# First token pair's transposes inside the last token tile's post products, and held-back q halves ahead of the last score block

## The chip, the cores and the metric

The kernel runs on one core of one Trainium2 chip (trn2). The metric is device time in microseconds, the median of three runs; the profile is of one further execution.

## The reference

Two layers over 512 tokens of width 1024, all in float32. Each layer does three sub-blocks on a residual stream `h`, and each sub-block starts with an RMS norm (pre) and ends with an RMS norm and the residual add (post):

- `h += 0.5 * rms(swiglu(rms(h)))`, with an inner width of 2816;
- `h += rms(mixer(rms(h)))`. One input projection feeds a short gated convolution, a Conformer convolution, differential attention (4 heads, two softmax maps per head, one subtracted from the other with a learned weight) and forgetting attention (8 heads). Each branch is mapped to width 1024, the gated sum of the four goes through an output projection `w_o`;
- a second `h += 0.5 * rms(swiglu(rms(h)))`.

## The kernel before

**Numbers and products.** Every float32 operand is split into a high part (rounded, ACT) and a low part (the rest, DVE), and every product is three matmuls: high by high, low by high, high by low (`mm3`, L128; `by_tokens`, L216). Weights come as one stream of 512 KB chunks; each is loaded by SP into `raw` (3 buffers), split by ACT into `wh` (L100) and by DVE into `wl` (L101), 5 buffers each. A chunk is 8 blocks of 128x128.

**The boundary between two sub-blocks** (`boundary`, L235) ends one and starts the next. It is reached seven times; the first has no post part (`post is None`, the input is loaded instead) and the last no pre part. The five between have both and are what the change touches. In each:

1. The post products run by tokens: for the second half of the channels, the last `HOLD` = 8 steps of the contraction are done token tile by token tile (L325 to L333). A tile of 128 tokens takes 8 steps of three matmuls, 24 matmuls of 512 columns.
2. After a tile's products come `gained` (square sums on ACT, `yg` on DVE), `update` (a reciprocal root `nr` on POOL, then the new residual `h` on DVE) and `normed` (square sums of `h` on ACT, another `nr` on POOL, then the normed rows `u` on DVE, L250). This chain is run for the four tiles one after the other while PE works on the next tile.
3. `turned` (L253) transposes the rows `u` of a pair of token tiles to channels by tokens: 16 PE transposes of 128x128 into four PSUM banks `pt` (four transposes each), and from each bank two pairs of copies: high part `xh` (ACT, L153) and low part `xl` (DVE, L146), each 128x256. Eight pairs in all for a token pair.
4. `outer(k, c)` (L272) does the first products of the next sub-block: for channel block k and one half of the tokens, four weight blocks by three matmuls of 256 columns, 12 matmuls, accumulated in four PSUM banks `pf`.

The order in the program is: products and chain of the four token tiles; `turned` for tiles 0 and 1; `outer` k = 0 to 5 for the first half; `turned` for tiles 2 and 3; `outer` k = 6 and 7 for the first half; `outer` k = 0 to 7 for the second half.

**Differential attention** (L585 to L630) runs four heads. Per head, `weights_of(i)` for the query blocks i = 0 to 3 makes two score blocks, their row minima (DVE, L517) and exponentials (ACT), and combines the two maps of block i - 1 (`combine`, DVE, L593 to L598, which ends with `e` at L597). The next head's query projection `q_of` stands between blocks 1 and 2. It puts two DVE operations that make the low halves of q (`qlo`, 64x512 each, L482) on the list `late`; the list is emptied by `settle`, which the next call of `group` does when its products are issued (L138, L123). That is `k_of` after block 3, where `combine` of block 3 is on the list behind them. `transposed` (L521) then turns the weights `e` by PE.

**What sets the order.** The kernel is written in a framework that plans: instructions of one engine are issued in an order that its planner derives from program order, its own costs and the buffers that are free. Buffers of one name come from one pool (`s`: 59 slots of 128x512 in SBUF, from which `xh`, `xl`, `u`, `yg`, `sq` all come; `p`: the 8 PSUM banks). In the loop of the four heads DVE alone is held to program order (`manual_schedule`, L585). Each engine works through its queue in order.

Of the kernel before, what the change touches and what calls it, by code (L numbers as in the profile page):

```python
# [22 lines left out]
NQ = T // P  # L23
# [18 lines left out]
HOLD = 8  # L42
# [12 lines left out]
def build(tc, ws, x, vecs, gains, wdf, lamv, fb, consts, out):  # L55
# [3 lines left out]
    with ExitStack() as ctx:  # L59
# [13 lines left out]
        def nm(s):  # L73
            cnt[0] += 1
            return f"{s}{cnt[0]}"
# [28 lines left out]
        def block(desc):  # L104
            i = len(order)
            order.append(desc)
            if i % CB == 0:
                c = i // CB
                for n in range(c, min(c + AHEAD + 1, NBLK // CB) if len(order) > 4 * KD else 0):
                    if n not in ready:  # L110
                        load(n)
                cur[:] = ready[c]
            j = (i % CB) * P
            return cur[0][:, j:j + P], cur[1][:, j:j + P]
# [4 lines left out]
        def settle():  # L119
            while late:  # L120
                late.pop(0)()
# [87 lines left out]
        def tile4(name, l, k, c):  # L209

            for j in range(4):
                block((name, l, k, c + P * j))
            b0 = (len(order) - 4) % CB * P
            return cur[0][:, b0:b0 + T], cur[1][:, b0:b0 + T]

        def by_tokens(out, x, t, w, first, last):  # L216

            r = slice(t * P, (t + 1) * P)
            PE.matmul(out=out, lhsT=x[0][:, r], rhs=w[0], start=first, stop=False)  # L219
            PE.matmul(out=out, lhsT=x[0][:, r], rhs=w[1], start=False, stop=False)  # L220
            PE.matmul(out=out, lhsT=x[1][:, r], rhs=w[0], start=False, stop=last)  # L221
# [10 lines left out]
        def squares(src, col):  # L232
            S.activation(out=slot(F32, "sq"), in_=src, func=AF.Square, accum_out=col)

        def boundary(post, pre, first):  # L235

            xs, pf, blk = [], [], []  # L240
            stat = np_.tile([P, 16], F32, tag="stat", name=nm("stat"))

            def normed(t):

                for c in range(2):
                    squares(hs[t][c], stat[:, 8 + 2 * t + c:9 + 2 * t + c])
                r = rstd_of([stat[:, 8 + 2 * t + c:9 + 2 * t + c] for c in range(2)])
                us = [slot(F32, "u") for _ in range(2)]
                for c in range(2):
                    V.tensor_scalar(out=us[c], in0=hs[t][c], scalar1=r, scalar2=None, op0=ALU.mult)  # L250
                return us

            def turned(us, h):  # L253

                c = HALVES[h]
                for b in range(4):
                    p = ps("pt")
                    for i in range(2):
                        k = 2 * b + i
                        for t in range(2):  # L260
                            o = k % 4 * P
                            PE.transpose(out=p[:, i * H + t * P:i * H + (t + 1) * P],
                                         in_=us[t][k // 4][:, o:o + P], identity=ident)
                    for i in range(2):
                        k = 2 * b + i
                        if len(xs) <= k:
                            xs.append((slot(F32R, "xh"), slot(F32R, "xl")))
                        g = vcol(pre[0], pre[1], k)
                        hi_of(xs[k][0][:, c], p[:, i * H:(i + 1) * H], g)
                        lo_of(xs[k][1][:, c], p[:, i * H:(i + 1) * H], xs[k][0][:, c], g)  # L270

            def outer(k, c):  # L272

                if not pf:
                    pf.extend(ps("pf") for _ in range(4))
                if len(blk) <= k:
                    blk.append([block(first[f][k]) for f in range(4)])
                x = (xs[k][0][:, c], xs[k][1][:, c])
                for f in range(4):
                    mm3(pf[f][:, c], blk[k][f], x, k == 0, k == KD - 1)  # L280

            us = []
            if post is None:
                for t in range(4):
                    for c in range(2):
                        nc.sync.dma_start(out=hs[t][c], in_=x[t * P:(t + 1) * P, c * T:(c + 1) * T])
                    load(t, 2 if t == 0 else 1)
                us = [normed(t) for t in range(4)]
            else:
                row, factor, name, l, ys = post  # L290
                n = len(ys)
                gb = gp.tile([P, D], F32, tag="gb", name=nm("gb"))
                nc.scalar.dma_start(out=gb, in_=gains[row:row + 1, :].broadcast_to([P, D]))
                yg = [[None, None] for _ in range(4)]

                def gained(t, c, p):
                    squares(p, stat[:, 2 * t + c:2 * t + c + 1])
                    yg[t][c] = slot(F32, "yg")
                    V.tensor_mul(out=yg[t][c], in0=p, in1=gb[:, c * T:(c + 1) * T])

                def update(t):
                    r = rstd_of([stat[:, 2 * t + c:2 * t + c + 1] for c in range(2)], factor)
                    for c in range(2):
                        V.scalar_tensor_tensor(out=hs[t][c], in0=yg[t][c], scalar=r, in1=hs[t][c],
                                               op0=ALU.mult, op1=ALU.add)
                        if pre is None:
                            (nc.sync, nc.scalar)[c].dma_start(out=out[t * P:(t + 1) * P, c * T:(c + 1) * T],
                                                              in_=hs[t][c])

                settle()  # L310
                py = [ps("py") for _ in range(4)]
                for k in range(n):
                    w = tile4(name, l, k, 0)
                    for t in range(4):
                        by_tokens(py[t], ys[k], t, w, k == 0, k == n - 1)
                    cover()
                for t in range(4):
                    gained(t, 0, py[t])
                py = [ps("py") for _ in range(4)]
                for k in range(n - HOLD):  # L320
                    w = tile4(name, l, k, T)
                    for t in range(4):
                        by_tokens(py[t], ys[k], t, w, k == 0, False)
                held = []
                for t in range(4):  # L325
                    for k in range(n - HOLD, n):
                        if t == 0:
                            held.append(tile4(name, l, k, T))
                        by_tokens(py[t], ys[k], t, held[k - n + HOLD], k == 0, k == n - 1)
                    gained(t, 1, py[t])  # L330
                    update(t)
                    if pre is not None:
                        us.append(normed(t))  # L333
                if pre is None:
                    return None
            turned(us[0:2], 0)
            for k in range(KD - 2):
                outer(k, HALVES[0])
            turned(us[2:4], 1)
            for k in range(KD - 2, KD):  # L340
                outer(k, HALVES[0])
            for k in range(KD):
                outer(k, HALVES[1])
            pf.append(group(first[4], xs))
            pf.append(group(first[5], xs))
            return xs, pf
# [35 lines left out]
        def mixer(l, entry):  # L382
# [198 lines left out]
            q, k = q_of(OFF_CQ), k_of(OFF_CK)  # L581
# [3 lines left out]
            with tc.manual_schedule(engines={mybir.EngineType.DVE}):  # L585
                for hd in range(4):
# [13 lines left out]
                    def weights_of(i):  # L600
                        for m in range(2):
                            exponentials(scores(q, k, m, i, False), es[m][i], bias[:, (NQ - 1 - i) * P:],
                                         sums[i][:, m:m + 1])
                        if i:
                            combine(i - 1)
# [3 lines left out]
                    weights_of(1)  # L609
                    q_next = q_of(cq)  # L610
                    weights_of(2)
                    weights_of(3)
                    late.append(lambda: combine(NQ - 1))
                    k_next = k_of(ck)
                    q, k = q_next, k_next
# [73 lines left out]
            for pr in range(4):  # L689
# [35 lines left out]
                if pr < 3:  # L725
                    q, k = nxt
# [54 lines left out]
        post = None  # L781
        for l in range(DEPTH):
            post = ffn(l, 1, boundary(post, ("ffn1_pre_g", l), ffn_first(l, 1)))
            post = mixer(l, boundary(post, ("mix_pre_g", l), mix_first(l)))
            post = ffn(l, 2, boundary(post, ("ffn2_pre_g", l), ffn_first(l, 2)))
# [51 lines left out]
```

## Time and profile before

| | before |
|---|---|
| median of 3 runs | 2795.95 us (2794.83 to 2796.22) |
| profiled execution, its own time | 2795.68 us |
| its span in the trace | 2793.9 us |
| PE (matmul) busy | 2720.7 us, 97% |
| DVE busy | 1392.6 us, 50% |
| ACT busy | 980.0 us, 35% |
| POOL busy | 75.7 us, 3% |
| weights and other data moved | 257.82 MB, mean 92 GB/s |

The profiled execution lies 0.27 us below the median of the runs, and 1.78 us of its time lie outside the span. PE is busy for nearly the whole span, so what counts is the 73.2 us in which it isn't, and the stretches in which it is busy at a lower clock.

### The profile page before, as it was taken

The page shows a single profiled execution, that of the slowest core. Times are in us where ns is not written, and L with a number is a line of the kernel's source. Part 1 is how long each engine was busy: PE and PEld are TensorE (multiplying, and loading weights), DVE is VectorE, ACT ScalarE, POOL GpSimd, SP SyncE. Part 2 cuts the span into 40 slices and gives each one's busy share as a digit, 9 for nine tenths or more (in the row PEclk, how much of TensorE's full clock was granted, in tenths as well). Part 3 has the DMA queues.
Part 4 walks back from the last instruction along what each step waited for, and adds up shares of the span by engine and source line. Part 5 has one row for each costly group of instructions (what it writes and reads, how often), then busy time and mean ns, then how long its engine had stood idle before and what let it go on. Part 6 is the DMA issues. An engine that isn't in the chain of part 4 may idle for free.

```text
span 2793.9 us, 32240 instructions
## 1 busy us (share of the span) xinstructions
PE 2720.7 (97%) x12884; PEld 2280.1 (82%) x12884; DVE 1392.6 (50%) x2287; ACT 980.0 (35%) x1607; POOL 75.7 (3%) x114
## 2 busy tenths in 40 slices
PE   7999989999999989999989999899999999899999
PEld 6888878887888878888888888888878888788887
DVE  4333248776775443332343332496777854433322
ACT  4222232354453333222242222324545533332221
POOL 0000000000000000000000000000000000000000
PEclk9999999999999999999999999999999999999999
DMA  4222223222222222222222222222222222232221
GB/s 153 97 98 98 98 70 109 88 76 68 95 84 95 98 83 98 94 95 99 83 98 99 98 98 97 87 94 81 76 84 87 84 94 98 70 112 95 95 98 68
DMA packets 73494, 257.82 MB, mean 92 GB/s; under 512 B 8432, under 2 KB 8816, under 8 KB 73344
## 3 DMA queue, kind: packets, MB, share of 16 engines
q1 hardware_dynamic: 68688, 246.45, 26.5%
q10 hardware_dynamic: 4656, 9.32, 1.0%
q8 instruction: 101, 1.65, 0.2%
q14 instruction: 49, 0.40, 0.0%
HBM read 253.60 MB, written 2.13 MB: 92 GB/s over the span
## 4 chain that ended last, share of the span: by engine, by line
PE 95%; DVE 3%; POOL 1%; issue 1%; DMA 0%; ACT 0%; ACTq 0%; POOLq 0%; DVEq 0%; SPq 0%
PE p L130 21%; PE p L132 21%; PE p L131 21%; PE py L220 6%; PE py L221 6%; PE py L219 6%; PE pf L131 2%; PE pf L132 2%; PE pf L130 2%; PE o L545 1%; PE pv L219 1%; PE pv L221 1%; PE pv L220 1%; PE pt L529 1%; POOL nr L229 1%; PE sc L499 1%
## 5 line engine op out<-in xcount | busy, mean ns | idle before, releaser
L100 ACT CAST wh<-raw 128x1024 fp32r<-128x1024 f32 (+1 forms) x465 | 488.7, 1051 | 1417.4 <-PE p L131 664.9
L101 DVE TENSOR_TENSOR wl<-raw,wh 128x1024 fp32r<-128x1024 f32 (+1 forms) x465 | 567.8, 1222 | 765.3 <-ACT wh L100 752.9
L130 PE MATMUL p<-xh,wh 128*128 128x512 f32 x2304 | 903.1, 392 | 0.0
L132 PE MATMUL p<-xh,wl 128*128 128x512 f32 x2304 | 898.0, 390 | 0.0
L131 PE MATMUL p<-xl,wh 128*128 128x512 f32 x2304 | 897.7, 390 | 0.0
L132 PEld LDWEIGHTS p<-xh,wl 128*128 128x128 f32 x2304 | 433.0, 188 | 91.0
L131 PEld LDWEIGHTS p<-xl,wh 128*128 128x128 f32 x2304 | 433.4, 188 | 89.0 <-issue 0.5
L130 PEld LDWEIGHTS p<-xh,wh 128*128 128x128 f32 x2304 | 433.6, 188 | 88.5 <-PE pt L529 0.5
L221 PE MATMUL py<-wh,gl 128*128 128x512 f32 x704 | 273.9, 389 | 0.0
L219 PE MATMUL py<-wh,gh 128*128 128x512 f32 x704 | 273.9, 389 | 0.0
L220 PE MATMUL py<-wl,gh 128*128 128x512 f32 x704 | 273.9, 389 | 0.0
L363 DVE TENSOR_TENSOR s<-p,s 128x512 f32<-128x512 f32 x80 | 55.3, 692 | 270.6 <-PE p L132 270.6
L392 DVE SCALAR_TENSOR_TENSOR yc<-ba,vec,yc 128x501 f32<-128x501 f32 (+17 forms) x240 | 169.7, 729 | 2.4
L219 PEld LDWEIGHTS py<-wh,gh 128*128 128x128 f32 x704 | 132.1, 188 | 27.6
L220 PEld LDWEIGHTS py<-wl,gh 128*128 128x128 f32 x704 | 132.1, 188 | 27.4
L221 PEld LDWEIGHTS py<-wh,gl 128*128 128x128 f32 x704 | 132.1, 188 | 27.3
L130 PE MATMUL pf<-xh,wh 128*128 128x256 f32 x384 | 115.0, 304 | 30.3 <-ACT xh L153 30.3
L131 PE MATMUL pf<-xl,wh 128*128 128x256 f32 x384 | 115.9, 302 | 9.6 <-DVE xl L146 9.6
L132 PE MATMUL pf<-xh,wl 128*128 128x256 f32 x384 | 114.7, 299 | 0.0
L130 PEld LDWEIGHTS pf<-xh,wh 128*128 128x128 f32 x384 | 79.6, 210 | 31.9 <-ACT xh L153 31.9
L519 ACT ACTIVATE e<-e,mx 128x128 f32<-128x128 f32 (+3 forms) x128 | 71.2, 557 | 60.0 <-DVE mx L517 48.4
L131 PEld LDWEIGHTS pf<-xl,wh 128*128 128x128 f32 x384 | 80.2, 209 | 11.4 <-DVE xl L146 11.4
(185 smaller groups left out, 2623.1 us busy)
## 6 DMA issues: line engine op xcount, KB each, us to landing
raw<-ws SPq DMA_DIRECT2D x463, 512.0 KB, 3.3
cb<-cum ACTq DMA_DIRECT2D x16, 256.0 KB, 3.5
gb<-gains ACTq DMA_DIRECT2D x6, 512.0 KB, 4.7
h<-x SPq DMA_DIRECT2D x8, 256.0 KB, 5.6
out<-h SPq DMA_DIRECT2D x4, 256.0 KB, 2.0
out<-h ACTq DMA_DIRECT2D x4, 256.0 KB, 2.0
raw<-ws SPq DMA_DIRECT2D x2, 256.0 KB, 7.1
cst<-consts ACTq DMA_DIRECT2D x1, 384.0 KB, 4.8
```

The costliest lines, as they stand in the source:

```text
L100: S.copy(out=wh[:, j], in_=raw[:, j])
L101: V.tensor_sub(out=wl[:, j], in0=raw[:, j], in1=wh[:, j].bitcast(F32))
L130: PE.matmul(out=out, lhsT=w[0], rhs=x[0], start=first, stop=False)
L131: PE.matmul(out=out, lhsT=w[0], rhs=x[1], start=False, stop=False)
L132: PE.matmul(out=out, lhsT=w[1], rhs=x[0], start=False, stop=last)
L219: PE.matmul(out=out, lhsT=x[0][:, r], rhs=w[0], start=first, stop=False)
L220: PE.matmul(out=out, lhsT=x[0][:, r], rhs=w[1], start=False, stop=False)
L221: PE.matmul(out=out, lhsT=x[1][:, r], rhs=w[0], start=False, stop=last)
L229: G.tensor_tensor(out=r, in0=var, in1=mhalf[:, 0:1], op=ALU.pow)
L363: V.tensor_mul(out=u, in0=pu, in1=x)
L392: V.scalar_tensor_tensor(out=acc[:, s:], in0=y[:, :T - s], scalar=vcol(wname, l, i * 4 + j), in1=acc[:, s:], op0=ALU.mult, op1=ALU.add)
L519: S.activation(out=e, in_=e, func=AF.Exp, scale=-1.0, bias=mx, accum_out=sums)
```

## The change

In `boundary`, `turned` for token tiles 0 and 1 is called inside the products of token tile 3, after four of its eight steps, where there is a post and a pre part. Where there is no post part (the first boundary) it stays where it was. In the differential attention, `settle()` is called ahead of `weights_of(3)`, so that the two `qlo` operations on the list stand before block 3 on DVE.

```diff
                     for k in range(n - HOLD, n):
                         if t == 0:
                             held.append(tile4(name, l, k, T))
+                        if t == NQ - 1 and k == n - HOLD // 2 and pre is not None:
+                            turned(us[0:2], 0)
                         by_tokens(py[t], ys[k], t, held[k - n + HOLD], k == 0, k == n - 1)
                     gained(t, 1, py[t])
                     update(t)
@@
                 if pre is None:
                     return None
-            turned(us[0:2], 0)
+            if post is None:
+                turned(us[0:2], 0)
             for k in range(KD - 2):
                 outer(k, HALVES[0])
             turned(us[2:4], 1)
@@
                     weights_of(1)
                     q_next = q_of(cq)
                     weights_of(2)
+                    settle()
                     weights_of(3)
                     late.append(lambda: combine(NQ - 1))
                     k_next = k_of(ck)
```

## Rows read from the trace of the kernel before

**Rows 1.** The page: the chain of work that ended last, shares of the span by engine.

```profile
PE 95%; DVE 3%; POOL 1%; issue 1%; DMA 0%; ACT 0%; ACTq 0%; POOLq 0%; DVEq 0%; SPq 0%
```

**Rows 2.** Who waited for whom, PE's rows: engine, tile and line that waited, what for, us in total, times, longest.

```profile
PE pf L130 <- ACT xh L153: 30.3, 6, 5.6
PE pt L262 <- DVE u L250: 14.8, 2, 11.9
PE pt L529 <- DVE e L597: 11.5, 4, 3.6
PE pf L131 <- DVE xl L146: 9.6, 6, 1.7
```

**Rows 3.** The timeline of PE at the second boundary (first SwiGLU block to mixer, layer 0): start, duration, engine, line, instruction, count, and in brackets the idle time before it and what ended it.

```profile
381.78 0.39 PE L219 MATMUL py<-wh,gh 128*128 128x512 f32 x1
...
387.23 1.91 PE L262 MATMUL pt<-cst,u 128*128 128x128 f32 x16
394.77 0.79 PE L130 MATMUL pf<-xh,wh 128*128 128x256 f32 x2 [5.63 <-ACT xh L153]
397.26 0.58 PE L131 MATMUL pf<-xl,wh 128*128 128x256 f32 x1 [1.70 <-DVE xl L146]
...
403.56 0.28 PE L131 MATMUL pf<-xl,wh 128*128 128x256 f32 x1
...
408.47 1.91 PE L262 MATMUL pt<-cst,u 128*128 128x128 f32 x16
410.14 0.36 PE L130 MATMUL pf<-xh,wh 128*128 128x256 f32 x1
```

**Rows 4.** The same timeline at the four other boundaries that have a post and a pre part: the two sets of transposes of each.

```profile
1026.79 1.91 PE L262 MATMUL pt<-cst,u 128*128 128x128 f32 x16
...
1047.39 1.91 PE L262 MATMUL pt<-cst,u 128*128 128x128 f32 x16
...
1400.85 1.91 PE L262 MATMUL pt<-cst,u 128*128 128x128 f32 x16
...
1420.57 1.91 PE L262 MATMUL pt<-cst,u 128*128 128x128 f32 x16
...
1774.02 1.91 PE L262 MATMUL pt<-cst,u 128*128 128x128 f32 x16
...
1794.83 1.91 PE L262 MATMUL pt<-cst,u 128*128 128x128 f32 x16
...
2412.95 1.91 PE L262 MATMUL pt<-cst,u 128*128 128x128 f32 x16
...
2433.41 1.91 PE L262 MATMUL pt<-cst,u 128*128 128x128 f32 x16
```

**Rows 5.** Windows of the second boundary: from and to, length, then busy time and count of PE, PEld, DVE, ACT and POOL, the granted clock of TensorE (1.00 is 2.4 GHz, 0.50 is 1.2 GHz), share and rate of the DMA engines.

```profile
392.20:393.20 1.00, 0.00 (x0) 0.00 (x0) 1.00 (x2) 0.23 (x1) 0.00 (x0) 1.00 0.85 291
393.20:394.20 1.00, 0.00 (x0) 0.00 (x0) 1.00 (x2) 1.00 (x4) 0.00 (x0) 0.51 0.91 332
...
397.30:403.40 6.10, 6.10 (x28) 6.10 (x29) 3.11 (x7) 4.22 (x8) 0.00 (x0) 0.50 0.12 35
...
408.50:414.00 5.50, 5.50 (x50) 5.50 (x49) 3.41 (x8) 3.28 (x8) 0.00 (x0) 1.00 0.00 0
```

**Rows 6.** The timeline of DVE at the second boundary, in order of time.

```profile
381.85 0.88 DVE L250 TENSOR_SCALAR u<-h,nr 128x512 f32<-128x512 f32 x2 [0.73 <-POOL nr L229]
...
385.52 2.38 DVE L101 TENSOR_TENSOR wl<-raw,wh 128x1024 fp32r<-128x1024 f32 x2
...
388.24 1.22 DVE L101 TENSOR_TENSOR wl<-raw,wh 128x1024 fp32r<-128x1024 f32 x1
389.90 0.88 DVE L250 TENSOR_SCALAR u<-h,nr 128x512 f32<-128x512 f32 x2 [0.44 <-POOL nr L229]
390.70 0.68 DVE L299 TENSOR_TENSOR yg<-py,gb 128x512 f32<-128x512 f32 x1
...
395.79 1.03 DVE L250 TENSOR_SCALAR u<-h,nr 128x512 f32<-128x512 f32 x2 [0.73 <-POOL nr L229]
...
397.75 0.87 DVE L146 SCALAR_TENSOR_TENSOR xl<-pt,vec,xh 128x256 fp32r<-128x256 f32 x2 [0.55 <-ACT xh L153]
399.17 0.88 DVE L146 SCALAR_TENSOR_TENSOR xl<-pt,vec,xh 128x256 fp32r<-128x256 f32 x2 [0.54 <-ACT xh L153]
...
409.62 2.92 DVE L146 SCALAR_TENSOR_TENSOR xl<-pt,vec,xh 128x256 fp32r<-128x256 f32 x7 [5.02 <-ACT xh L153]
```

**Rows 7.** Differential attention of layer 0, fourth head: DVE's timeline from the last score block on, then PE's last transposes of that head.

```profile
676.74 0.69 DVE L517 CUSTOM_DVE_ANT_0 e<-sc,bias 128x512 f32<-128x512 f32 x1 [2.77 <-PE pt L529]
...
679.87 1.38 DVE L146 SCALAR_TENSOR_TENSOR qlo<-p,qh 64x512 fp32r<-64x512 f32 x2
...
682.20 0.75 DVE L597 SCALAR_TENSOR_TENSOR e<-e,sums,e 128x512 f32<-128x512 f32 x1
...
683.01 1.12 PE L529 MATMUL pt<-cst,e 128*128 128x128 f32 x4 [3.59 <-DVE e L597]
```

**Rows 8.** The same of the second head: `qlo` on DVE, the transposes on PE; and the window after the fourth head's last transposes.

```profile
603.64 1.38 DVE L146 SCALAR_TENSOR_TENSOR qlo<-p,qh 64x512 fp32r<-64x512 f32 x2
...
606.34 1.42 PE L529 MATMUL pt<-cst,e 128*128 128x128 f32 x10
...
683.80:687.00 3.20, 3.20 (x10) 2.58 (x9) 3.12 (x4) 1.03 (x3) 0.00 (x0) 0.54 0.32 108
```

## The prediction

> **What bounds the kernel now.** I read the chain of waits first: 95% of the span is PE [rows 1], so time is gained only where PE stands still or runs slowly. Then the waits of PE [rows 2]: almost all of its idle time has four causes, and three of them are touched by the change. `pf` waits for `xh` 30.3 us and for `xl` 9.6 us, six times each, which is once per boundary; `pt` in the attention waits for `e` 11.5 us. (The 14.8 us of `pt` waiting for `u` hold one wait of 11.9 us, at the start of the program, which stays.) Then PE's timeline at one boundary [rows 3]: the products of tile 3 run from 381.78 to 387.23, 24 of them, 0.227 us each; the 16 transposes follow; PE stands 5.63 us until the first `xh`, does two matmuls, stands 1.70 us until the first `xl`, and comes to the second set of transposes at 408.47. Last the windows: the granted clock is 1.00 at 392.2 and 0.5 from 393.2, some 4 us after PE fell idle, and still 0.50 to 403.4 [rows 5]. So the pause is paid twice, once standing and once at 1.2 GHz.
>
> The reason of the pause is on DVE [rows 6]. The first pair's `u` are ready at 381.85 + 0.88 = 382.7, but the transposes sit behind tile 3's products, and the first `xl` sits on DVE behind the whole chain of tile 3, whose `u` ends at 396.8.
>
> **The boundaries: what can be had.** The two sets of transposes lie 21.24 us apart here [rows 3], and 20.60, 19.72, 20.81 and 20.46 at the others [rows 4]: 102.8 us in all. PE's work in it is 16 transposes, 1.67 us (408.47 to 410.14), and 72 matmuls of `outer` at 0.120 (41 from 403.56 to 408.47), 8.6 us: 10.3 us. So 102.8 - 5 x 10.3 = 51.3 us is the ceiling. Per boundary that is 7.3 us of standing and 2.8 us of slow clock (70 matmuls took 408.47 - 397.26 = 11.2 us instead of 8.4).
>
> **What takes the place of the pause.** I work it out at the second boundary, in the clock of rows 3. The transposes now stand after half of tile 3, at 384.5, and wait for `u` of tile 1, ready at 382.7: the added wait costs nothing, and if that margin of 1.8 us were gone, the 12 remaining products would queue behind it. They take 1.67 us, so tile 3's products end at 388.9. No DMA is issued by `turned` and none is moved; SP's queue is passed by nothing. On POOL the `nr` of tiles 2 and 3 keep their places.
>
> On ACT and DVE eight pairs of copies now come ahead of tile 3's chain. All tiles of the `s` pool seem to get their slots in program order: at present the first `xl` follows both `u` of tile 3 although its transposes had long been done. So I expect DVE's queue as: `wl`, `wl` (385.5 to 387.8), the two `u` of tile 2, `xl` 0 to 7, then `yg` of tile 3. The `u` started at 389.9 and may come up to 0.9 earlier, as the `wl` at 388.24 now comes later; I take 389.0, and the first `xl` runs from 389.9 to 390.3. PE has done two matmuls by then and loses 390.3 - 388.9 - 0.24 = 1.2 us; bounds 0 and 2.1 (both ends of that 0.9, or the first `xl` ahead of the `u`).
>
> Then `outer` 0 to 5 need one `xl` per 12 matmuls, 1.44 us. The copies come at 1.42 us per two (397.75 to 399.17) [rows 6], so they stay ahead, and PE is through at 390.3 + 70 x 0.12 = 398.7.
>
> Now the second pair. The first pair's copies take between 7 x 0.42 = 2.9 us (the second set, `x7` at 409.62) and 4 x 1.42 = 5.7 us (the first set, ACT and DVE in turns) [rows 6]. I take 5.7, since slots given out in order keep them in order. The rows show idle DVE of 0.55 us in each bank's turn, while `xh` of the same bank runs. The Trainium skill, PSUM — Partial Sum Buffer, section "PSUM bank collisions raise a hardware error", says that two engines must not be in one bank at once, reads against reads included. By that rule the two engines can overlap only between banks, and the price of this change is the 5.7 us; by the second set's rate alone it would be 2.9 us and the fourth tile 2.8 us earlier, which changes the sum of the first rival below by 5 x 2.8 = 14 us and that of the forecast by under 1 us a boundary.
>
> So `xl` 7 ends at about 389.9 + 5.7 = 395.6, and one or two `wl` (1.14 us each, partly in the 0.55 us gaps) push `yg` of tile 3 to about 396.2. From `yg` to the end of `u` it was 396.8 - 390.7 = 6.1 us: `u` is ready at 402.3. Bounds: 397 if the copies are quick and the `wl` come after, 404 if both `wl` and a late start count in full.
>
> PE is free at 398.7, 3.6 us before that. What it does there decides. `outer` 6 and 7 of the first half need only the first pair; if the planner sees the same lag as I do, it sets these 24 matmuls (2.9 us) and the 8 transposes of tile 2 (0.8 us) into the gap. PE then stands no longer than some tenths, the 8 transposes of tile 3 end at 403.2, and with the first copies behind them the second half starts near 403.8. Before, it started at 410.14 + 24 x 0.12 = 413.0. That is a gain of 9.2 here. Over five boundaries: before 102.8 + 5 x 4.55 = 125.6 from the end of tile 3's products to the second half, after 5 x (403.8 - 387.2) = 83: 42.6 us, no low clock left.
>
> **The attention.** In the fourth head PE waits 3.59 us for the last `e`, which ends at 682.95 [rows 7]. Ahead of it on DVE stand the two `qlo`, 1.38 us. After the change they run ahead of the last score block, where DVE now stands 2.77 us anyway, so `e` and PE's last four transposes come 1.38 us earlier. The clock is 0.54 in the window behind [rows 8], and if it returns at the same moment, half of that is lost: 0.7 to 1.4 us per layer, 2 us for both. In the other heads the ten transposes run without a wait [rows 8], and `qlo` moves from ahead of `combine` of block 3 to ahead of block 3: the sum of DVE's work to that `e` is the same, so nothing. If the exponentials of block 3 became the last thing, the cost would be up to 1.38 us in six heads, 8 us.
>
> **Sum.** 42.6 + 2 = 44 us from 2795.7 of the profiled execution, 0.3 under the median of the runs: 2752 us in terms of the median.
>
> **Rivals.**
>
> *PE waits for the second pair instead.* The planner leaves `outer` 6 and 7 behind the second transposes. Then PE stands from 398.7 to 402.3, the transposes and the 24 matmuls end at 402.3 + 4.55 = 406.9, and 125.6 - 5 x 19.6 = 27.5 us are gained: 2766 with the attention. The clock fell about 4 us after PE fell idle [rows 5], so it may fall here too, at up to 2.8 us each, 14 us: 2766 to 2780. For it: that order is the program's. Against: the lag is long enough to be seen by any plan.
>
> *The copies stay behind.* If the planner puts `xh` and `xl` behind tile 3's chain all the same, PE waits for 396.8 as now, and the move does nothing: 2794. Against it: in program order they now come first.
>
> *DVE becomes the bound, and it is slower than before.* Copies, weight splits and three chains share DVE; its gaps from 385.5 on are under 1 us each [rows 6]. If `u` of tile 3 came later than 408.5, PE would reach the second pair later than now. From there each microsecond costs 5 us: at 410 the kernel takes 2795.9 + 5 x 1.5 - 2 = 2801. `yg` would have to start at 402.4, 6 us later than worked out; nothing in the rows is that long.
>
> **How the numbers follow.** The forecast has 55% (2743 to 2760), PE waiting for the second pair 36% (2760 to 2780), copies behind 6%, DVE slower 3%. The low end is the ceiling: 2795.9 - 51.3 - 2.8 = 2742. The high end 2778 leaves out the last of the second case and the cases near or above the old time, about a tenth, and the low one next to nothing. What a measurement can tell from no change is 0.2%, 5.6 us. Faster 0.93: the forecast, the second case and a part of the third (the attention and a boundary or two may still gain); same 0.04: the rest of the third; slower 0.03.
>
> **What would show it.** Right: `pf` waiting for `xh` near 2 us in total (the first boundary alone) and for `xl` about 1 us per boundary; no granted clock of 0.5 at the boundaries; 16 transposes in the middle of tile 3's products; 96 instead of 72 matmuls of `pf` ahead of tile 3's transposes; in the fourth head `qlo` ahead of the last score block and the wait of `pt` for `e` 1.4 us shorter. Wrong: a wait of `pt` for `u` of 3 us and more at each boundary (the second case), `xl` behind `u` of tile 3 on DVE, or a wait of `pt` in the first three heads.

## The result and the profile after

The changed kernel takes 2761.33 us (median of 4 runs, 2758.96 to 2762.70), the kernel before 2796.09 us beside it (4 runs, 2794.83 to 2797.39): a ratio of 0.9875, 95% interval 0.9858 to 0.9892. The profiled execution took 2762.70 us, its span is 2760.9 us, 33.0 less than before. Forecast were 2752 us, and 2742 to 2778 as the range.

PE's waits after, in the columns of [rows 2]:

```profile
PE pt L262 <- DMA raw<-ws: 11.9, 1, 11.9
PE pf L131 <- DVE xl L146: 8.8, 6, 1.5
PE pt L532 <- DVE e L600: 8.7, 4, 2.2
PE pf L130 <- ACT xh L153: 3.1, 6, 2.2
PE pt L262 <- DVE u L250: 3.0, 1, 3.0
```

Against [rows 2], the wait for `xh` fell from 30.3 to 3.1 us, and 2.2 of that stand at the first boundary, which the change does not touch. The wait for `xl` hardly fell, 9.6 to 8.8: it is a wait of 1.47 where one of 1.70 was. The wait of 11.9 us at the start of the program is the one that [rows 2] put down to `u`; its releaser changed its name, not its length. The 3.0 us for `u` stand at the first boundary too. At the five changed boundaries PE waited for no `u` longer than 0.1 us.

The second boundary on PE, the place of [rows 3] (this trace's clock runs 0.39 us ahead of that one: tile 3's products start at 382.17 here and at 381.78 there):

```profile
382.17 0.39 PE L219 MATMUL py<-wh,gh 128*128 128x512 f32 x1
...
384.89 1.91 PE L262 MATMUL pt<-cst,u 128*128 128x128 f32 x16
...
389.15 0.39 PE L221 MATMUL py<-wh,gl 128*128 128x512 f32 x1
389.73 0.61 PE L130 MATMUL pf<-xh,wh 128*128 128x256 f32 x3 [0.20 <-ACT xh L153]
391.81 0.39 PE L131 MATMUL pf<-xl,wh 128*128 128x256 f32 x1 [1.47 <-DVE xl L146]
...
393.43 0.36 PE L130 MATMUL pf<-xh,wh 128*128 128x256 f32 x1 [0.28 <-DVE xl L146]
...
393.87 0.41 PE L131 MATMUL pf<-xl,wh 128*128 128x256 f32 x1
...
397.07 0.37 PE L130 MATMUL pf<-xh,wh 128*128 128x256 f32 x1
...
402.19 0.60 PE L262 MATMUL pt<-cst,u 128*128 128x128 f32 x4
...
404.07 1.47 PE L262 MATMUL pt<-cst,u 128*128 128x128 f32 x12
...
418.21 0.28 PE L132 MATMUL pf<-xh,wl 128*128 128x256 f32 x1
```

The 16 transposes stand inside tile 3's products and wait for nothing; the 5.63 us of standing are gone. Of the second set, four transposes and 12 matmuls of `outer` went ahead, and 12 transposes follow. From the start of tile 3's products to the last product of `outer` it is 418.21 - 382.17 = 36.04 us, 42.71 before (381.78 to 424.49). The windows there, in the columns of [rows 5]:

```profile
391.00:393.90 2.90, 1.81 (x13) 1.63 (x14) 2.68 (x5) 1.50 (x4) 0.00 (x0) 0.99 0.73 244
394.00:397.40 3.40, 3.40 (x19) 3.40 (x17) 2.09 (x5) 2.24 (x6) 0.00 (x0) 0.52 0.57 183
397.50:402.10 4.60, 4.60 (x41) 4.60 (x40) 2.53 (x7) 1.49 (x6) 1.02 (x2) 1.00 0.43 140
```

The low clock is not gone but shorter: some 3.4 us at 0.5 (394.0 to 397.4) where 10.2 were (393.2 to 403.4, [rows 5]), and PE is busy in all of it. From 393.87 to 397.07 it starts 15 matmuls, one every 0.213 us instead of 0.120. For the 16 that fit into 3.4 us that costs 16 x 0.093 = 1.5 us. In this profiled execution the low clock stands at four of the five boundaries.

DVE in the same stretch, the place of [rows 6]:

```profile
385.90 2.38 DVE L101 TENSOR_TENSOR wl<-raw,wh 128x1024 fp32r<-128x1024 f32 x2
...
389.35 0.88 DVE L250 TENSOR_SCALAR u<-h,nr 128x512 f32<-128x512 f32 x2 [0.73 <-POOL nr L229]
390.14 1.22 DVE L101 TENSOR_TENSOR wl<-raw,wh 128x1024 fp32r<-128x1024 f32 x1
391.28 0.48 DVE L146 SCALAR_TENSOR_TENSOR xl<-pt,vec,xh 128x256 fp32r<-128x256 f32 x1
391.68 1.22 DVE L101 TENSOR_TENSOR wl<-raw,wh 128x1024 fp32r<-128x1024 f32 x1
392.81 0.87 DVE L146 SCALAR_TENSOR_TENSOR xl<-pt,vec,xh 128x256 fp32r<-128x256 f32 x2
394.22 0.88 DVE L146 SCALAR_TENSOR_TENSOR xl<-pt,vec,xh 128x256 fp32r<-128x256 f32 x2 [0.54 <-ACT xh L153]
395.64 0.88 DVE L146 SCALAR_TENSOR_TENSOR xl<-pt,vec,xh 128x256 fp32r<-128x256 f32 x2 [0.54 <-ACT xh L153]
...
397.63 0.69 DVE L299 TENSOR_TENSOR yg<-py,gb 128x512 f32<-128x512 f32 x1
...
402.22 1.03 DVE L250 TENSOR_SCALAR u<-h,nr 128x512 f32<-128x512 f32 x2 [0.73 <-POOL nr L229]
```

The queue is the predicted one with one exception: a weight split at 390.14 stands ahead of the first `xl`, and another ahead of the second.

In the attention, the place of [rows 7], the wait that was 3.59 us:

```profile
675.36 1.12 PE L532 MATMUL pt<-cst,e 128*128 128x128 f32 x4 [2.17 <-DVE e L600]
```

Where the 33.0 us came from follows by measuring each boundary as above, from the start of tile 3's products to the last product of `outer`, in the timelines (us, in order of time; "low" marks a stretch at clock 0.5; the other kernels are those of the experiments below; sums and differences are taken before rounding):

```
                          2nd        3rd        4th        5th        6th       sum
before                  42.71 low  42.07 low  41.19 low  42.27 low  41.92 low  210.2
changed kernel          36.05 low  35.87 low  36.04 low  34.85      35.81 low  178.6
move_only               36.12 low  35.52 low  34.95      34.83      35.45      176.9
settle_only             42.37 low  42.23 low  41.31 low  42.32 low  42.26 low  210.5
copies_first            34.54      34.53      34.48      34.53      34.57      172.7
spread_banks            34.57      36.02 low  34.48      35.73 low  35.75 low  176.6
copies_first_spread     33.05      33.08      33.07      33.05      33.19      165.4
pe_in_order             36.64 low  36.61 low  36.59 low  36.63 low  36.61 low  183.1
six_of_eight            34.94      34.79      35.95 low  34.79      35.19      175.7
```

The boundaries gave 210.2 - 178.6 = 31.5 us. Of the rest, the two stretches between boundaries that hold the differential attention are 0.6 and 1.3 us shorter, and the start of the program up to the second boundary is 0.4 us longer. Each row is one profiled execution, so differences of a microsecond or two between rows are not those of the medians: the profiled execution is the longest run of the changed kernel and the shortest of `copies_first_spread`. PE's own work in one is 31.8 us (24 products of 0.227, two sets of transposes of 1.67, 192 matmuls of 0.12).

### The profile page after: what moved, and what is told of

Its sections match the earlier page's. It is cut to its first block, busy times and chain, and to the rows that moved or that the text cites. A ratio compares the mean times of both kernels' runs of the same rounds, so it can differ in the third digit from the quotient of the medians.

```text
span 2760.9 us, 32249 instructions
## 1 busy us (share of the span) xinstructions
PE 2717.1 (98%) x12884; PEld 2274.7 (82%) x12884; DVE 1392.6 (50%) x2287; ACT 980.1 (35%) x1607; POOL 71.5 (3%) x114
## 4 chain that ended last, share of the span: by engine, by line
PE 95%; DVE 2%; ACT 1%; issue 1%; DMA 1%; POOL 1%; POOLq 0%; DVEq 0%; ACTq 0%
PE p L130 21%; PE p L132 21%; PE p L131 21%; PE py L219 6%; PE py L220 6%; PE py L221 6%; PE pf L131 2%; PE pf L132 2%; PE pf L130 2%; PE o L548 1%; PE pv L219 1%; PE pv L220 1%; PE pv L221 1%; PE pt L532 1%; PE sc L502 1%; DVE wl L101 1%
```

## The experiments

Forecast and result differ by 9 us, and both parts of the change act at once. So the questions were: what is each part worth; which of two moments on DVE costs the rest, the first `xl` or `u` of tile 3; and does it matter what the planner puts into the gap. The kernels that follow are the changed one with the edit shown, except `settle_only`.

**The two parts alone.** `move_only` leaves the attention as before; `settle_only` is the kernel before with this line alone:

```
+                    settle()
                     weights_of(3)
```

> The first pair's transposes inside tile 3's products, without the settle ahead of the last score block. Theory (the gain is the boundaries' and the attention adds 1.4 us per layer, one wait of 0.7 to 1.4 us less): five boundaries as in the changed kernel, pt waiting for e 11.5 us as before, and about 2763 us. Rival (the two parts depend on each other, or the settle is worth several us through the clock): over 2768, or boundaries that differ from the changed kernel's.

> The settle alone, transposes where they were. Theory: boundaries as before with 7.3 us of standing each; pt waiting for e 8.7 us instead of 11.5; 2793 to 2795 us, within 0.2% of before. Rival (q's low halves ahead of the score block delay the exponentials of all heads): slower, pt waiting in the first three heads too.

`move_only`: 2762.68 us (2761.40 to 2764.58), ratio 0.9881 (0.9866 to 0.9895). `settle_only`: 2794.48 us (2792.67 to 2795.41), ratio 0.9993 (0.9983 to 1.0002), beside 2796.56 before. In the trace of `settle_only` the wait of `pt` is the changed kernel's, and the waits of `pf` are those of [rows 2]:

```profile
PE pt L529 <- DVE e L597: 8.7, 4, 2.2
```

So the move carries all but some 2 us. The time alone, whose interval reaches 1.0002, could not show the attention's 2 us, and the runs of `move_only` and of the changed kernel overlap. The wait shows it, 11.5 to 8.7 us, and so do the two stretches with the attention: in the seven traces with the `settle` they are together 1.0 to 3.1 us shorter than before, in `move_only` 0.3.

**The first pair's copies ahead of the third tile's normalisation.** `copies_first`: `normed(2)` is called behind `turned` in the program, so that `u` of tile 2 does not stand ahead of the first `xl` on DVE.

```
                         if t == NQ - 1 and k == n - HOLD // 2 and pre is not None:
                             turned(us[0:2], 0)
+                            us.append(normed(2))
...
-                    if pre is not None:
+                    if pre is not None and t != 2:
                         us.append(normed(t))
```

> In the changed kernel tile 2's normed rows are made after the first pair's copies instead of before, so that the first xl stands on DVE right behind two weight splits. Theory of two bounds (the wait for the first xl and the lag of tile 3's rows are nearly equal in length, so taking away one leaves the other): PE no longer waits 1.5 us for xl, but waits 1 to 2 us for u of tile 3 before the second transposes; 2756 to 2762 us, a gain of at most 5 on the changed kernel. Rival (only the wait for the first xl and the slow clock behind it remain, 3.9 us per boundary): both go, 2742 to 2745 us.

2756.27 us (2756.01 to 2756.65), ratio 0.9857 (0.9842 to 0.9872). PE and DVE at the second boundary:

```profile
398.14 0.70 PE L262 MATMUL pt<-cst,u 128*128 128x128 f32 x3 [0.17 <-DVE u L250]
...
403.47 1.20 PE L262 MATMUL pt<-cst,u 128*128 128x128 f32 x9 [1.35 <-DVE u L250]
```

```profile
387.94 0.48 DVE L146 SCALAR_TENSOR_TENSOR xl<-pt,vec,xh 128x256 fp32r<-128x256 f32 x1
...
402.88 1.03 DVE L250 TENSOR_SCALAR u<-h,nr 128x512 f32<-128x512 f32 x2 [0.73 <-POOL nr L229]
```

Tile 3's products start at 381.94 in this trace. The first `xl` starts 6.0 us after that instead of 9.1 (391.28 - 382.17), and PE no longer waits for it; no boundary has a low clock. In the columns of [rows 5]:

```profile
393.00:401.80 8.80, 8.54 (x69) 7.97 (x68) 5.29 (x15) 4.34 (x13) 1.10 (x2) 1.00 0.45 148
```

But `u` of tile 3 starts 20.9 us after the start of tile 3's products, 0.9 later than without the edit (402.22 - 382.17 = 20.1), and now PE, being early, stands 1.35 us for it. That is the theory of two bounds: the wait for the first `xl` had hidden most of the other.

**Neighbouring blocks in different banks.** `spread_banks`: bank `b` holds the blocks `b` and `b + 4` instead of `2b` and `2b + 1`, and the copies go through the blocks in order, so that two that follow each other lie in two banks.

```
-                        k = 2 * b + i
+                        k = b + 4 * i
...
+                for k in range(KD):
+                    p, i = pts[k % 4], k // 4
...
+                    hi_of(xs[k][0][:, c], p[:, i * H:(i + 1) * H], g)
+                    lo_of(xs[k][1][:, c], p[:, i * H:(i + 1) * H], xs[k][0][:, c], g)
```

> In the changed kernel the eight channel blocks of a pair are spread over the four PSUM banks so that neighbours in order lie in different banks; the work is the same. Theory (high and low copy of one bank take turns, 1.42 us per bank, and that is because they share a bank): the first set's xl come at 0.42 to 0.45 us each, and u of tile 3 is ready about 1.6 us earlier; the wait for the first xl stays, so only the second wait of 0.28 us goes and the time falls by 1 to 2 us to about 2760. Rival (the copies take turns for another reason): still 1.42 us per two. Rival (the lag of tile 3 bounds the stretch): 2753 us.

2759.61 us (2759.07 to 2761.18), ratio 0.9868 (0.9852 to 0.9885). DVE, then PE:

```profile
392.51 2.83 DVE L146 SCALAR_TENSOR_TENSOR xl<-pt,vec,xh 128x256 fp32r<-128x256 f32 x7
395.25 0.68 DVE L301 TENSOR_TENSOR yg<-py,gb 128x512 f32<-128x512 f32 x1
...
399.82 1.02 DVE L250 TENSOR_SCALAR u<-h,nr 128x512 f32<-128x512 f32 x2 [0.73 <-POOL nr L229]
```

```profile
391.51 0.39 PE L131 MATMUL pf<-xl,wh 128*128 128x256 f32 x1 [1.46 <-DVE xl L146]
...
400.33 1.99 PE L264 MATMUL pt<-cst,u 128*128 128x128 f32 x16
```

Seven `xl` take 2.83 us without a gap, 0.40 each, where the changed kernel needs 1.42 for two; `u` of tile 3 starts 399.82 - 381.86 = 18.0 us after the start of tile 3's products (381.86 in this trace), 2.1 us earlier than in the changed kernel. So ACT and DVE had taken turns because two neighbouring blocks lay in one bank. That agrees with the Trainium skill, PSUM — Partial Sum Buffer, section "PSUM bank collisions raise a hardware error", by which two engines must not be in one bank at once. PE still stands 1.46 us for the first `xl`, and the median is only 1.7 us lower; the runs of the two kernels overlap, so the time by itself does not show a gain.

**Both together.** `copies_first_spread` has the last two edits.

> Both edits together: the first pair's copies ahead of the third token tile's normalisation, and neighbouring channel blocks in different banks. Theory of two bounds (first the first xl, then u of tile 3 against PE): with the copies first alone the first xl came 1.4 us earlier and PE then stood 1.5 us a boundary for u of tile 3 (the boundaries took 34.5 us); with the banks spread alone u of tile 3 came 1.9 us earlier, and PE still stood 1.5 us for the first xl. With both, neither wait is left, no low clock at a boundary, and each boundary goes from 34.5 to 32.0-33.2 us: 2756.3 minus 5 x 1.3 to 2.5 gives 2744 to 2750 us. Rival (one bound only: the two edits save the same microseconds twice): 2755 to 2757 us with boundaries of 34.5 us. Rival (DVE is the bound, by the sum of its work before u of tile 3): a wait of pt for u of 1 us and more stays, 2752 to 2756 us.

2749.37 us (5 runs, 2747.49 to 2751.97), ratio 0.9834 (0.9821 to 0.9847): the fastest of the kernels here. PE at the second boundary, then two windows:

```profile
388.42 0.28 PE L130 MATMUL pf<-xh,wh 128*128 128x256 f32 x1
...
392.44 0.36 PE L130 MATMUL pf<-xh,wh 128*128 128x256 f32 x1 [0.75 <-DVE xl L146]
...
400.50 1.58 PE L264 MATMUL pt<-cst,u 128*128 128x128 f32 x12
```

```profile
388.00:392.00 4.00, 3.69 (x29) 3.41 (x27) 3.34 (x6) 3.13 (x8) 0.00 (x0) 1.00 0.84 260
392.00:400.00 8.00, 7.56 (x63) 7.59 (x64) 5.12 (x16) 3.30 (x11) 1.78 (x4) 1.00 0.65 195
```

PE goes from the products into `outer` without a stop and stands once, 0.75 us. The boundaries take 165.4 us; the two edits alone saved 6.0 and 2.1 of the changed kernel's 178.6, together 13.2. By the medians of the runs it is 5.1, 1.7 and 12.0. So the savings more than add, as with two bounds in series: with the copies first alone PE came early and stood for `u`, with the banks spread alone `u` came early and PE still stood for the first `xl`. The rivals, one bound or the sum of DVE's work, are out (they had 2752 to 2757).

**PE held to the program's order.** `pe_in_order`:

```
-            for k in range(KD - 2):
-                outer(k, HALVES[0])
+            with tc.manual_schedule(engines={mybir.EngineType.PE}):
+                for k in range(KD - 2):
+                    outer(k, HALVES[0])
...
```

> The changed kernel with PE held to the program's order from the first outer products to the end of the post block (no matmul of outer 6 and 7 ahead of the second transposes). Theory (the hoisted 12 matmuls and the four early transposes of tile 2 fill what would be standing): PE then stands for u of tile 3 at each boundary, 1.5 + 0.4 us more than now, 3 us where the clock falls behind it: boundaries of 38 to 39 us instead of 35.8, and 2761 + 10 to 16 = 2771 to 2777 us, with a wait of pt for u of 15 us or more in all. Rival (the hoisting is worth nothing, since PE is late there anyway): 2759 to 2763 us with no wait for u.

2766.66 us (2765.99 to 2767.64), ratio 0.9896 (0.9880 to 0.9912).

```profile
402.27 0.27 PE L262 MATMUL pt<-cst,u 128*128 128x128 f32 x1
402.96 1.86 PE L262 MATMUL pt<-cst,u 128*128 128x128 f32 x15 [0.42 <-DVE u L250]
```

The result lies between theory and rival. The hoisting is worth (183.1 - 178.6) / 5 = 0.9 us a boundary, half of what was expected of it: PE comes to the second transposes at 402.27, and stands 0.42 us for `u` (0.55 to 0.61 at the other boundaries). There was nearly no gap to fill, since PE itself was late. (The low clock stands at all five boundaries here, at four in the changed kernel, and the wait for the first `xl` is 1.69 us instead of 1.47; both are part of the 0.9.)

**The transposes later.** `six_of_eight` sets them ahead of the last quarter of tile 3's held products:

```
-                        if t == NQ - 1 and k == n - HOLD // 2 and pre is not None:
+                        if t == NQ - 1 and k == n - 2 and pre is not None:
```

> The changed kernel with the 16 transposes later inside tile 3's products: with a quarter of the held products left behind them instead of half. The transposes end 0.8 to 0.9 us later. Theory (the first xl is late because of what stands ahead of it on DVE, two weight splits and tile 2's u, not because of the transposes): the first xl ends when it did and the time is 2759 to 2764 us. Rival (the chain transposes, xh, xl sets the first xl): it comes 0.8 us later at each of five boundaries, 2764 to 2767 us.

2761.70 us (2759.74 to 2762.74), ratio 0.9876 (0.9862 to 0.9890): no change.

```profile
387.00 1.91 PE L262 MATMUL pt<-cst,u 128*128 128x128 f32 x16
...
392.36 0.39 PE L131 MATMUL pf<-xl,wh 128*128 128x256 f32 x1 [1.73 <-DVE xl L146]
```

```profile
391.03 0.88 DVE L250 TENSOR_SCALAR u<-h,nr 128x512 f32<-128x512 f32 x2 [0.44 <-POOL nr L229]
391.83 0.48 DVE L146 SCALAR_TENSOR_TENSOR xl<-pt,vec,xh 128x256 fp32r<-128x256 f32 x1
```

Counted from the start of tile 3's products (382.92 here), the transposes start 1.4 us later than in the changed kernel, 4.1 us after it instead of 2.7 (expected was a shift of 0.8 to 0.9), and the first `xl` starts 8.9 us after it instead of 9.1, right behind `u` on DVE: it is DVE's queue that sets it. (This kernel's profiled execution, 2759.74 us, is its fastest run; the 3.0 us that its boundaries save against the changed kernel are the difference of the two profiled executions, not of the medians.)

## Why the prediction was right, and what it mis-sized

**Right: the bound and the mechanism.** PE's standing at the boundary was put down to the first pair's copies behind tile 3's chain; with the copies ahead of it the 5.63 us went. The transposes inside the products wait for nothing. Tile 3's products ended, in the clock of [rows 3], at 389.0 (389.38 - 0.39), forecast 388.9.

**Right: DVE's queue and the bank's turns.** `xl` came at 1.42 us per two, as taken; `yg` of tile 3 at 397.2 and its `u` at 402.9 (403.25 - 0.39), forecast 396.2 and 402.3.

**Right: the attention.** `e` came earlier by the two `qlo`: PE's wait went from 3.59 to 2.17, 1.42 us for a forecast of 1.38; `move_only` against the changed kernel, and `settle_only` against the kernel before, differ by 1.4 and 2.1 us in the median, forecast 2. No wait showed in the other heads.

**Mis-sized: the wait for the first `xl`.** The step said that DVE runs the two `u` of tile 2 and then the copies, and that PE loses 1.2 us, bounds 0 and 2.1. The weight split of 388.24, rightly seen to come later, went in behind `u` but ahead of the first `xl`, which so ended 1.1 us later than worked out (391.76 - 0.39 = 391.4 for 390.3); another split went in ahead of the second `xl`. PE stands 0.20 + 1.47 + 0.28 = 1.95 us: 0.75 more, within the bounds.

**Wrong: "no low clock left".** The step that failed is this term of the sum: the low clock was put at nothing. The prediction gives no reason for it; the nearest is the row in its first rival, where the clock fell some 4 us after PE fell idle. It fell after 1.95 us of standing in three pieces too, for some 3.4 us, at four of five boundaries. Where it did, the boundary took 35.8 to 36.05 us, and 34.85 where it did not, 1.1 us less; by the matmuls' own pace it costs 1.5 us. In `copies_first` and `copies_first_spread`, where the wait for the first `xl` is gone or halved, it fell at none.

**What this made of the sum.** Forecast was 42.71 - 9.2 = 33.5 us for the second boundary and 210.2 - 42.6 = 167.6 for the five; measured are 36.05 and 178.6. The 11 us missing are 2.2 a boundary: 0.75 of standing, 0.9 (four fifths of 1.1) to 1.2 (four fifths of 1.5) of low clock; the rest, 0.3 to 0.5, was not followed up. The two copies' edits take the low clock and most of the standing away and bring 165.4, about the forecast's own boundary. So the measured 2761 us lies outside the band that the prediction gave to its forecast, 2743 to 2760, and in the one that it gave to its first rival, 2760 to 2780, though that rival's wait for the second pair was not there: the range held in part because it was made wide for another cause.

**The gap for the planner.** PE was to be free at 398.7 and to fill 3.6 us with `outer` 6 and 7. It came to the second transposes at 401.8 (402.19 - 0.39), about 1 us ahead of `u`; the planner set half of these matmuls, 12, ahead, so that 84 instead of the forecast 96 stand before tile 3's transposes. That decided little (`pe_in_order`, 0.9 us a boundary). The first rival, PE waiting for the second pair, would have had PE stand 3.6 us; with its very order PE stood 0.42 to 0.61 us. Its time, 2766 to 2780, holds `pe_in_order`, but for another reason: the standing at the first `xl` and the low clock. The other rivals, copies behind and DVE as the bound, did not show: the copies ran ahead of tile 3's chain, and in no kernel with the move was a boundary as long as before; the longest stop for `u` of tile 3 seen is the 1.36 us in `copies_first`.

## What to carry to other kernels

When a stall is removed by moving its source forward, work out the next two waits in series, not the next one: here the waits for the first `xl` and for `u` of tile 3 stood one behind the other, and edits worth 5.1 and 1.7 us alone (medians) were worth 12.0 together. Instructions that wait in a queue and are moved past must be given a new place one by one; the split that "comes later" landed ahead of the critical copy. Where two engines copy from one PSUM bank by turns, give neighbours different banks: 0.40 us per copy against 0.71.

## What the runs showed of the hardware that was not expected

The granted clock fell to 0.5 behind much less standing than before, 1.95 us in three pieces instead of 5.63 in one. At the fifth boundary PE stood for the same 0.20, 1.47 and 0.28 us as at the second, and there it did not fall (two of the waits, then the window of the whole boundary):

```profile
1757.93 0.61 PE L130 MATMUL pf<-xh,wh 128*128 128x256 f32 x3 [0.20 <-ACT xh L153]
1760.02 0.38 PE L131 MATMUL pf<-xl,wh 128*128 128x256 f32 x1 [1.47 <-DVE xl L146]
...
1750.00:1786.00 36.00, 33.96 (x254) 31.87 (x253) 23.94 (x49) 20.25 (x39) 3.38 (x7) 1.00 0.32 108
```

In `move_only`, whose boundaries are written the same, a wait of 1.46 us was followed by a low clock at two of five. In `spread_banks` the same wait was followed by one at three of five boundaries, in `pe_in_order` (1.69 us) at five, in `six_of_eight` (1.73 us at the second) at one. What tells these apart stays open; no run was made for it. What is shown is that there was none at ten boundaries in two kernels where PE no longer stood more than 0.83 us for an `xl`, though it stood up to 1.36 us for `u` in one of them. The mean granted clock of every run, profiled or not, fits this: 0.998 in all four of `copies_first`, 0.997 to 0.998 in the five of `copies_first_spread`, 0.995 to 0.996 in the four of the changed kernel.

On POOL, `nr` of tile 2 took 1.48 us before, beside a weight split on DVE that had begun at 388.24 [rows 6], and 0.55 after, when the split came behind `u`; in `six_of_eight` a split stands beside it again, and it took 1.49:

```profile
388.39 1.48 POOL L229 TENSOR_TENSOR nr<-nw,mhalf 128x1 f32<-128x1 f32 x1 [4.23 <-DVE nw L228]
```

```profile
388.76 0.55 POOL L229 TENSOR_TENSOR nr<-nw,mhalf 128x1 f32<-128x1 f32 x1 [4.22 <-DVE nw L228]
```

```profile
389.51 1.49 POOL L229 TENSOR_TENSOR nr<-nw,mhalf 128x1 f32<-128x1 f32 x1 [4.22 <-DVE nw L228]
```

The first line is of the kernel before, the second of the changed one, the third of `six_of_eight`. So this operation took 0.93 us longer beside a split. Each of the three traces has 48 `nr` of this kind: five of them took 1.5 us in the kernel before and in `six_of_eight`, all five begun while a split ran, and the others, and all 48 of the changed kernel, 0.5 to 0.6. That is consistent with the Trainium skill, SBUF — State Buffer, section "SBUF: two separate sides", by which the two engines share a pair of ports, and a DVE operation with two SBUF inputs, as the split has in `raw` and `wh`, or the one on POOL holds it for the whole instruction; no run here tried it by itself.
